# A PSUM bank set aside for the running sum of the convolution taps

## The chip, the core and the metric

The kernel runs on one core of a Trainium2 chip. TensorE (PE) multiplies matrices into PSUM; VectorE (DVE), ScalarE (ACT) and GpSimd (POOL) work on tiles of 128 partitions; SyncE (SP) issues the transfers. Each engine takes its instructions in a fixed order and waits at semaphores for others. The metric is the device time of one execution in microseconds; lower is better.

## What is computed

One layer of a diffusion block over 512 tokens of width 1024, in float32, with 256 context tokens. Cut to what matters here:

```python
def conformer_conv(conv_in, w_dw, b_dw, ln_g, ln_b, w_pw):
    a, g = jnp.split(conv_in, 2, axis=-1)
    u = a * jax.nn.sigmoid(g)
    u = depthwise_conv(u, w_dw, width=31) + b_dw        # 1024 channels, one filter each
    return jax.nn.silu(layer_norm(u, ln_g, ln_b)) @ w_pw

def block(x, ctx, ...):
    hx = modulate(rms_norm(x), ...)                     # adaLN
    conv_x, qa, kva, kr, gates = split(hx @ w_in)
    att = softmax(q @ k.T) @ v                          # 8 heads, low-rank q and kv, rotary part
    x = x + m * ((sig(g1) * conv(conv_x) + sig(g2) * att @ w_o) @ w_out)
    return rms_norm(x + m2 * swiglu(modulate(rms_norm(x))))
```

The 31-tap depthwise convolution of conv_x and the eight heads of attention are independent of each other until the branches are merged.

## The kernel before

Activations lie transposed: 128 channels on the partitions, 512 tokens along the free axis, so 1024 channels are eight tiles. Every product of matrices is made of three matmuls (mm3), since weights and activations are split into a high and a low part; the high part is copied out of PSUM by ACT and the low part is the difference, taken by DVE (split, L103 to L105; split_scaled, L99 to L101, for the queries). Weights are split in the same way: w_hi on ACT (L121), w_lo on DVE (L125).

PSUM has eight banks. ps_s takes two pairs of them for the scores. ps_x takes the other four in rotation, for everything else.

The program opens with a part in an order written out by hand (to about 140 us). Then come the heads (L755 to L773). Head h makes its scores and softmax (scores, p), in between the matmuls of one convolution tile (conv_steps: g and a into two ps_x banks, then u = a*sigmoid(g) on DVE, L333), then prepares the next head (prep: queries into px, split by L100 and L101; keys kx and context keys kc into px, split by L104 and L105; in even heads also the rotary part and the values), then attends (attend): for six blocks of keys four transposes of p into a bank pt (L486), its split into ph and pl, and three matmuls into the bank po.

The taps of convolution tile i (conv_taps) stand in the source with a priority lowered by 3000 (later, L80), so the scheduler places them where an engine would else be free; the order it arrives at is then fixed. Five tiles go over ACT (a scaled copy per tap, L351, three buffers) and POOL (the sum, L352). The tiles 1, 4 and 7 (DVE_TILES) go over DVE alone: L344 begins the sum, 29 instructions of L346 carry it on in a PSUM bank acc, and the last one writes it to the SBUF slot a:

```python
acc = ps_x() if i in DVE_TILES else a
```

That bank comes out of the rotation of ps_x. After the heads come the gates, the normalisation of the convolution, the merging, and the feed-forward part. ap is the pool of SBUF slots for activations; its 60 slots are handed out by slot().

Of the kernel before, what the change touches and what calls it, by code (L numbers as in the profile page):

```python
# [10 lines left out]
F32 = mybir.dt.float32  # L11
# [7 lines left out]
P = 128  # L19
# [27 lines left out]
DVE_TILES = (1, 4, 7)  # L47
# [14 lines left out]
def block_kernel(ctx: ExitStack, tc: tile.TileContext, I, out):  # L62
# [2 lines left out]

    cp = ctx.enter_context(tc.tile_pool(name="cp", bufs=1))
    wp = ctx.enter_context(tc.tile_pool(name="wp", bufs=3))
    ap = ctx.enter_context(tc.tile_pool(name="ap", bufs=60))
    tp = ctx.enter_context(tc.tile_pool(name="tp", bufs=3))
    sm = ctx.enter_context(tc.tile_pool(name="sm", bufs=4))  # L70
    bp = ctx.enter_context(tc.tile_pool(name="bp", bufs=4))
    pp = ctx.enter_context(tc.tile_pool(name="pp", bufs=1, space=PSUM))
# [3 lines left out]
    def nm(s):  # L76
        count[0] += 1
        return f"{s}{count[0]}"
# [7 lines left out]
    def slot(dt=F32, n=512):  # L86
        return ap.tile([P, n], dt, tag="act", name=nm("a"))
# [66 lines left out]
    def v(name, i=None, n=1):  # L154
        a, b = VEC[name]
        return vec[:, a:b] if i is None else vec[:, a + i:a + i + n]
# [21 lines left out]
    def spread(r, nb, psp):  # L178
        dg = temp(nb * P)
        dve.tensor_tensor(  # L180
            out=dg.rearrange("p (b j) -> p b j", b=nb),
            in0=ident.unsqueeze(1).to_broadcast([P, nb, P]),
            in1=r.unsqueeze(2).to_broadcast([P, nb, P]), op=ALU.mult)
        bc = psp(nb * P)
        pe.matmul(bc, lhsT=ones, rhs=dg, start=True, stop=True)
        return bc
# [4 lines left out]
                      start=first and b == 0, stop=last and b == nb - 1)  # L191

    def ps_x(n=512):
        return pp.tile([P, 512], F32, tag="x", name=nm("px"), bufs=4)[:, 0:n]

    def ps_s():
        return pp.tile([P, 1024], F32, tag="s", name=nm("ps"), bufs=2)
# [47 lines left out]


    ab = (ps_s(), ps_s())
    accx = [ab[j // 2][:, (j % 2) * 512:(j % 2) * 512 + 512] for j in range(4)] + [ps_x(), ps_x()]
    tiny = ps_x

    def slab(k, kc):
# [83 lines left out]
    def conv_taps(i, u):  # L335
        a = slot()
        conv[i] = a
        acc = ps_x() if i in DVE_TILES else a
        for j in range(TAPS):
            wcol = wdw[:, i * TAPS + j:i * TAPS + j + 1]  # L340
            src = u[:, j:j + S]
            if i in DVE_TILES:
                if j == 0:
                    dve.tensor_scalar(out=acc, in0=src, scalar1=wcol, scalar2=v("b_dw", i), op0=ALU.mult, op1=ALU.add)  # L344
                else:
                    dve.scalar_tensor_tensor(out=a if j == TAPS - 1 else acc, in0=src, scalar=wcol, in1=acc, op0=ALU.mult, op1=ALU.add)  # L346
            elif j == 0:
                act.activation(a, src, AF.Identity, scale=wcol, bias=v("b_dw", i))
            else:
                t = bp.tile([P, S], F32, tag="tap", name=nm("tap"), bufs=3)  # L350
                act.activation(t, src, AF.Copy, scale=wcol)  # L351
                pool.tensor_tensor(out=a, in0=a, in1=t, op=ALU.add)  # L352
# [164 lines left out]
    with tc.manual_schedule(engines={ET.PE, ET.DVE, ET.Activation, ET.Pool, ET.SP}):  # L517
# [26 lines left out]
        bc = spread(r, 4, tiny)  # L544
# [73 lines left out]
            return dg  # L618

        def bcast(dg, n):  # L620
            bc = tiny(n)
            pe.matmul(bc, lhsT=ones, rhs=dg, start=True, stop=True)
            o = slot(n=n)
            act.copy(o, bc)
            return o
# [125 lines left out]
    with later(TAPS_LATER):  # L751
        conv_taps(0, u0)
        conv_taps(1, u1)
# [24 lines left out]
    if True:  # L778
# [22 lines left out]
        for h in range(H):  # L801
            a, b = slot(F32R), slot(F32R)
            split(o_t[h], a, b)
            oa.append((a, b))
        bc = spread(rstd_cols(st, D, 4), 4, ps_x)
        yc = []
        for i in range(KD):
# [3 lines left out]
            a, b = slot(F32R), slot(F32R)  # L811
# [12 lines left out]
        for i in range(KD):  # L824
# [6 lines left out]
            a, b = slot(F32R), slot(F32R)  # L831
# [197 lines left out]
        i = KD - 1  # L1029
# [139 lines left out]
```

## Time and profile before

| | us |
|---|---|
| median of three runs | 1095.37 (1094.88 to 1096.67) |
| the profiled execution, its time | 1095.09 |
| its span | 1093.3 |
| PE busy | 972.0 |
| DVE busy | 640.0 |
| ACT busy | 525.4 |
| POOL busy | 283.8 |

The span is the time between the first and the last instruction that the profiler recorded; 1.8 us of the execution's time lie outside it. Busy time is the time in which an engine had at least one instruction under way. For matmuls the end is modelled, so the row of PE says where it had nothing at all to do and not how full it was.

### The profile page before, as it was taken

The page shows a single profiled execution, that of the slowest core. Times are in us where ns is not written, and L with a number is a line of the kernel's source. Part 1 is how long each engine was busy: PE and PEld are TensorE (multiplying, and loading weights), DVE is VectorE, ACT ScalarE, POOL GpSimd, SP SyncE. Part 2 cuts the span into 40 slices and gives each one's busy share as a digit, 9 for nine tenths or more (in the row PEclk, how much of TensorE's full clock was granted, in tenths as well). Part 3 has the DMA queues.
Part 4 walks back from the last instruction along what each step waited for, and adds up shares of the span by engine and source line. Part 5 has one row for each costly group of instructions (what it writes and reads, how often), then busy time and mean ns, then how long its engine had stood idle before and what let it go on. Part 6 is the DMA issues. An engine that isn't in the chain of part 4 may idle for free.

```text
span 1093.3 us, 13176 instructions
## 1 busy us (share of the span) xinstructions
PE 972.0 (89%) x4772; PEld 812.0 (74%) x4772; DVE 640.0 (59%) x1052; ACT 525.4 (48%) x963; POOL 283.8 (26%) x237
## 2 busy tenths in 40 slices
PE   8789990988199962999999999999999999999996
PEld 8677880766187752777887888988888888888886
DVE  6997894465846568443589686483653333333333
ACT  4566686888168971554437223353333323332222
POOL 3766168998109991000000000020000000000000
PEclk9889995989599995999999999999999999999998
DMA  9801320011011000123363865133542223333312
GB/s 340 295 20 47 97 74 28 13 58 29 19 32 39 22 20 0 39 95 98 97 211 121 262 205 198 63 99 99 178 133 100 98 86 96 92 95 98 106 54 78
DMA packets 40721, 107.54 MB, mean 98 GB/s; under 512 B 4432, under 2 KB 6736, under 8 KB 40656
## 3 DMA queue, kind: packets, MB, share of 16 engines
q1 hardware_dynamic: 40656, 106.70, 30.3%
q8 instruction: 37, 0.61, 0.2%
q14 instruction: 28, 0.23, 0.1%
HBM read 104.59 MB, written 2.10 MB: 98 GB/s over the span
## 4 chain that ended last, share of the span: by engine, by line
PE 65%; DVE 13%; POOL 8%; ACT 8%; issue 5%; DMA 0%; POOLq 0%; SPq 0%; DVEq 0%; ACTq 0%
PE px L137 12%; PE px L138 11%; PE px L139 11%; POOL a L352 8%; PE ps L138 7%; PE ps L139 7%; PE ps L137 7%; DVE px L346 4%; DVE gm L263 2%; ACT tap L351 2%; PE ps L468 2%; DVE wl L125 2%; ACT p L477 1%; PE px L319 1%; ACT p L474 1%
## 5 line engine op out<-in xcount | busy, mean ns | idle before, releaser
L125 DVE TENSOR_TENSOR wl<-wr,wh 128x512 fp32r<-128x512 f32 (+1 forms) x264 | 197.2, 755 | 238.7 <-ACT wh L121 235.9
L121 ACT CAST wh<-wr 128x512 fp32r<-128x512 f32 (+2 forms) x274 | 164.5, 608 | 295.0 <-PE px L138 141.8
L137 PE MATMUL px<-a,wh 128*128 128x512 f32 (+1 forms) x607 | 224.2, 371 | 1.6 <-DVE t L417 1.0
L352 POOL TENSOR_TENSOR a<-a,tap 128x512 f32<-128x512 f32 x150 | 202.1, 1348 | 86.3 <-ACT tap L351 58.9
L138 PE MATMUL px<-a,wh 128*128 128x512 f32 (+1 forms) x607 | 223.1, 368 | 1.2 <-DVE a L722 1.1
L139 PE MATMUL px<-a,wl 128*128 128x512 f32 (+1 forms) x607 | 222.7, 367 | 0.0
L175 POOL TENSOR_TENSOR s<-s,mhalf 128x2 f32<-128x2 f32 (+1 forms) x10 | 9.3, 932 | 687.5 <-DVE s L173 687.5
L138 PE MATMUL ps<-a,wh 128*128 128x512 f32 (+1 forms) x376 | 141.6, 376 | 0.9 <-DVE a L921 0.8
L137 PE MATMUL ps<-a,wh 128*128 128x512 f32 (+1 forms) x376 | 141.5, 376 | 0.0
L139 PE MATMUL ps<-a,wl 128*128 128x512 f32 (+1 forms) x376 | 141.2, 375 | 0.0
L137 PEld LDWEIGHTS px<-a,wh 128*128 128x128 f32 x607 | 114.3, 188 | 22.1 <-ACT a L104 1.5
L138 PEld LDWEIGHTS px<-a,wh 128*128 128x128 f32 x607 | 114.4, 188 | 21.7 <-DVE a L722 2.0
L139 PEld LDWEIGHTS px<-a,wl 128*128 128x128 f32 x607 | 114.3, 188 | 18.9
L351 ACT ACTIVATE tap<-u,wdw 128x512 f32<-128x512 f32 x150 | 105.1, 722 | 33.8 <-POOL a L352 30.0
L138 PEld LDWEIGHTS ps<-a,wh 128*128 128x128 f32 x376 | 70.7, 188 | 14.3 <-DVE a L921 1.5
L319 PE MATMUL px<-a,wh 128*128 128x512 f32 x256 | 80.7, 393 | 0.0
L139 PEld LDWEIGHTS ps<-a,wl 128*128 128x128 f32 x376 | 70.8, 188 | 12.8
L137 PEld LDWEIGHTS ps<-a,wh 128*128 128x128 f32 x376 | 70.8, 188 | 12.6
L468 PE MATMUL ps<-a,a 128*128 128x512 f32 x160 | 60.1, 411 | 12.8 <-ACT a L104 12.8
L486 PE MATMUL px<-cst,p 128*128 128x128 f32 x192 | 30.7, 288 | 42.6 <-DVE a L346 42.2
L346 DVE SCALAR_TENSOR_TENSOR px<-u,wdw,px 128x512 f32<-128x512 f32 x87 | 65.6, 754 | 2.7
L486 PEld LDWEIGHTS px<-cst,p 128*128 128x128 f32 x192 | 25.2, 150 | 47.6 <-DVE a L346 42.6
(196 smaller groups left out, 1436.2 us busy)
## 6 DMA issues: line engine op xcount, KB each, us to landing
wr<-in_w_dram SPq DMA_DIRECT2D x60, 512.0 KB, 3.5
wr<-in_w_in_dram SPq DMA_DIRECT2D x35, 512.0 KB, 3.6
p<-in_w_mod_dram SPq DMA_DIRECT2D x64, 256.0 KB, 4.1
a<-in_w_mod_dram SPq DMA_DIRECT2D x32, 256.0 KB, 5.7
wr<-in_w_o_dram SPq DMA_DIRECT2D x8, 512.0 KB, 5.2
wr<-in_w_pw_dram SPq DMA_DIRECT2D x8, 512.0 KB, 5.6
wr<-in_w_out_dram SPq DMA_DIRECT2D x8, 512.0 KB, 3.7
a<-in_xT_dram SPq DMA_DIRECT2D x13, 256.0 KB, 5.6
```

Of the source, the lines that this page charges most:

```text
L121: act.copy(h, raw[:, i * WB:i * WB + h.shape[-1]])
L125: (eng or dve).tensor_tensor(out=l, in0=raw[:, i * WB:i * WB + h.shape[-1]], in1=h.bitcast(F32), op=ALU.subtract)
L137: pe.matmul(ps, lhsT=wh, rhs=ah, start=first, stop=False)
L138: pe.matmul(ps, lhsT=wh, rhs=al, start=False, stop=False)
L139: pe.matmul(ps, lhsT=wl, rhs=ah, start=False, stop=last)
L263: dve.scalar_tensor_tensor(out=gm[k], in0=slab(k, kc), scalar=sc[:, kc:kc + 1], in1=gm[k], op0=ALU.mult, op1=ALU.add)
L319: pe.matmul(ps, lhsT=l, rhs=r, start=k == 0 and i == 0, stop=k == n - 1 and i == 2)
L346: dve.scalar_tensor_tensor(out=a if j == TAPS - 1 else acc, in0=src, scalar=wcol, in1=acc, op0=ALU.mult, op1=ALU.add)
L351: act.activation(t, src, AF.Copy, scale=wcol)
L352: pool.tensor_tensor(out=a, in0=a, in1=t, op=ALU.add)
L468: pe.matmul(s[:, 0:512], lhsT=l[:, q0:q0 + P], rhs=rx_, start=i == 0, stop=i == 4)
L486: pe.transpose(pt[:, qb * P:(qb + 1) * P], ps_[qb][:, kb * P:(kb + 1) * P], ident)
```

## The change

A second PSUM tag, c, gets one bank (ps_c), and the tag x of ps_x keeps three instead of four. Three users go to the new bank: the running sum of the taps of the tiles 1, 4 and 7, the last of the six sums of the opening projection (accx[5]), and the four broadcasts in the part written by hand (bcast). The pool of activations has 64 slots instead of 60.

```diff
-    ap = ctx.enter_context(tc.tile_pool(name="ap", bufs=60))
+    ap = ctx.enter_context(tc.tile_pool(name="ap", bufs=64))
...
     def ps_x(n=512):
-        return pp.tile([P, 512], F32, tag="x", name=nm("px"), bufs=4)[:, 0:n]
+        return pp.tile([P, 512], F32, tag="x", name=nm("px"), bufs=3)[:, 0:n]
+
+    def ps_c():
+        return pp.tile([P, 512], F32, tag="c", name=nm("pc"))
...
-    accx = [...] + [ps_x(), ps_x()]
+    accx = [...] + [ps_x(), ps_c()]
...
-        acc = ps_x() if i in DVE_TILES else a
+        acc = ps_c() if i in DVE_TILES else a
...
         def bcast(dg, n):
-            bc = tiny(n)
+            bc = ps_c()[:, 0:n]
```

No instruction is added or removed. The scheduler orders the heads anew, and the lines behind L194 move down by three (L346 becomes L349, L486 becomes L489).

DVE at tile 4, in head 2. u_2388 is the tile's input, px_2503 (then pc_2503) its running sum, wl the low parts of weights, px_2545, px_2559 and px_2570 the query, key and context key of head 3. Before:

```order
L333 SCALAR_TENSOR_TENSOR u_2388<-t_2462,px_2464 128x512
L125 TENSOR_TENSOR wl_2775<-wr_2770,wh_2773 128x512
L344 TENSOR_SCALAR px_2503<-u_2388,wdw,vec 128x512
L346 SCALAR_TENSOR_TENSOR px_2503<-u_2388,wdw,px_2503 128x512 x5
L125 TENSOR_TENSOR wl_2903<-wr_2899,wh_2901 128x512
L125 TENSOR_TENSOR wl_2904<-wr_2899,wh_2902 128x512
L346 SCALAR_TENSOR_TENSOR px_2503<-u_2388,wdw,px_2503 128x512 x24
L346 SCALAR_TENSOR_TENSOR a_2502<-u_2388,wdw,px_2503 128x512
L101 SCALAR_TENSOR_TENSOR a_2556<-px_2545,a_2555 128x512
L105 TENSOR_TENSOR a_2567<-px_2559,a_2566 128x512
```

And now:

```order
L336 SCALAR_TENSOR_TENSOR u_2388<-t_2462,px_2464 128x512
L347 TENSOR_SCALAR pc_2503<-u_2388,wdw,vec 128x512
L125 TENSOR_TENSOR wl_2775<-wr_2770,wh_2773 128x512
L349 SCALAR_TENSOR_TENSOR pc_2503<-u_2388,wdw,pc_2503 128x512 x3
L125 TENSOR_TENSOR wl_2903<-wr_2899,wh_2901 128x512
L125 TENSOR_TENSOR wl_2904<-wr_2899,wh_2902 128x512
L349 SCALAR_TENSOR_TENSOR pc_2503<-u_2388,wdw,pc_2503 128x512 x26
L349 SCALAR_TENSOR_TENSOR a_2502<-u_2388,wdw,pc_2503 128x512
L101 SCALAR_TENSOR_TENSOR a_2556<-px_2545,a_2555 128x512
L105 TENSOR_TENSOR a_2567<-px_2559,a_2566 128x512
```

Two of the taps moved from ahead of the second and third weight split to behind them; the splits of query and key stand behind the last tap in both.

ACT at tile 1, in head 0. tap are the scaled copies that POOL sums, a_1679 begins the sum of tile 2, a_1791 is the high part of the next query, a_1802 and a_1813 those of the keys, ph_1822 that of the first transposed block. Before:

```order
L351 ACTIVATE tap_1684<-u_1565,wdw 128x512
L351 ACTIVATE tap_1687<-u_1565,wdw 128x512
L348 ACTIVATE a_1679<-u_1565,vec,wdw 128x512
L100 ACTIVATE a_1791<-px_1781 128x512
L104 CAST a_1802<-px_1795 128x512
L104 CAST ph_1822<-px_1817 128x512
L104 CAST a_1813<-px_1806 128x256
L351 ACTIVATE tap_1690<-u_1565,wdw 128x512
```

And now:

```order
L354 ACTIVATE tap_1684<-u_1565,wdw 128x512
L351 ACTIVATE a_1679<-u_1565,vec,wdw 128x512
L100 ACTIVATE a_1791<-px_1781 128x512
L354 ACTIVATE tap_1687<-u_1565,wdw 128x512
L104 CAST a_1802<-px_1795 128x512
L354 ACTIVATE tap_1690<-u_1565,wdw 128x512
L104 CAST a_1813<-px_1806 128x256
L354 ACTIVATE tap_1693<-u_1565,wdw 128x512
L104 CAST ph_1822<-px_1817 128x512
```

One tap moved from ahead of a_1679 and of the query's copy to behind them, and taps now stand between the copies that follow.

DVE at tile 7, in head 5. t_3683 and t_3685 are the rotary products of head 6's query (px_3673), pl their low parts. Before:

```order
L344 TENSOR_SCALAR px_3631<-u_3516,wdw,vec 128x512
L125 TENSOR_TENSOR wl_4004<-wr_3999,wh_4002 128x512
L346 SCALAR_TENSOR_TENSOR px_3631<-u_3516,wdw,px_3631 128x512
L417 TENSOR_TENSOR t_3683<-px_3673,cst 128x512
L417 TENSOR_TENSOR t_3685<-px_3673,cst 128x512
L346 SCALAR_TENSOR_TENSOR px_3631<-u_3516,wdw,px_3631 128x512
L105 TENSOR_TENSOR pl_3688<-t_3683,ph_3687 128x512
L105 TENSOR_TENSOR pl_3692<-t_3685,ph_3691 128x512
L125 TENSOR_TENSOR wl_4005<-wr_3999,wh_4003 128x512
L346 SCALAR_TENSOR_TENSOR px_3631<-u_3516,wdw,px_3631 128x512 x27
L346 SCALAR_TENSOR_TENSOR a_3630<-u_3516,wdw,px_3631 128x512
L101 SCALAR_TENSOR_TENSOR a_3706<-px_3695,a_3705 128x512
```

And now:

```order
L125 TENSOR_TENSOR wl_4004<-wr_3999,wh_4002 128x512
L347 TENSOR_SCALAR pc_3631<-u_3516,wdw,vec 128x512
L420 TENSOR_TENSOR t_3683<-px_3673,cst 128x512
L420 TENSOR_TENSOR t_3685<-px_3673,cst 128x512
L349 SCALAR_TENSOR_TENSOR pc_3631<-u_3516,wdw,pc_3631 128x512
L105 TENSOR_TENSOR pl_3688<-t_3683,ph_3687 128x512
L105 TENSOR_TENSOR pl_3692<-t_3685,ph_3691 128x512
L125 TENSOR_TENSOR wl_4005<-wr_3999,wh_4003 128x512
L349 SCALAR_TENSOR_TENSOR pc_3631<-u_3516,wdw,pc_3631 128x512 x28
L349 SCALAR_TENSOR_TENSOR a_3630<-u_3516,wdw,pc_3631 128x512
L101 SCALAR_TENSOR_TENSOR a_3706<-px_3695,a_3705 128x512
```

One tap moved from ahead of the rotary low parts to behind them.

## Rows read from the trace of the kernel before

**Rows 1.** Page, busy us, share of the span, instructions of each engine

```profile
PE 972.0 (89%) x4772; PEld 812.0 (74%) x4772; DVE 640.0 (59%) x1052; ACT 525.4 (48%) x963; POOL 283.8 (26%) x237
```

**Rows 2.** Waits: who waited for whom; us in total, times, longest

```profile
PE px L486 <- DVE a L346: 42.2, 2, 27.4
PE px L432 <- DVE a L346: 28.5, 1, 28.5
...
PE ps L468 <- ACT a L104: 12.8, 2, 11.3
```

**Rows 3.** Windows: length, busy PE, PEld, DVE, ACT, POOL, granted clock, DMA share, GB/s

```profile
163.00:178.00 15.00, 0.24 (x2) 0.13 (x2) 12.30 (x16) 8.80 (x13) 14.21 (x11) 0.64 0.20 66
...
268.60:296.30 27.70, 0.32 (x3) 0.11 (x1) 24.84 (x33) 5.16 (x9) 8.70 (x9) 0.58 0.13 38
402.50:431.00 28.50, 0.07 (x1) 0.00 (x0) 25.14 (x32) 7.46 (x13) 12.24 (x9) 0.57 0.00 0
```

**Rows 4.** Page, groups of instructions: busy us, mean ns, idle before, releaser

```profile
L352 POOL TENSOR_TENSOR a<-a,tap 128x512 f32<-128x512 f32 x150 | 202.1, 1348 | 86.3 <-ACT tap L351 58.9
...
L346 DVE SCALAR_TENSOR_TENSOR px<-u,wdw,px 128x512 f32<-128x512 f32 x87 | 65.6, 754 | 2.7
```

**Rows 5.** Timeline of ACT at tile 1: start, length, instruction, idle before

```profile
186.53 0.72 ACT L351 ACTIVATE tap<-u,wdw 128x512 f32<-128x512 f32 x1 [0.62 <-POOL u L331]
187.87 0.72 ACT L351 ACTIVATE tap<-u,wdw 128x512 f32<-128x512 f32 x1 [0.62 <-POOL a L352]
188.50 0.80 ACT L348 ACTIVATE a<-u,vec,wdw 128x512 f32<-128x512 f32 x1
189.20 0.57 ACT L100 ACTIVATE a<-px 128x512 fp32r<-128x512 f32 x1
```

**Rows 6.** Timeline of POOL behind tile 1

```profile
189.37 21.73 POOL L352 TENSOR_TENSOR a<-a,tap 128x512 f32<-128x512 f32 x16 [1.45 <-ACT a L348]
211.55 8.50 POOL L352 TENSOR_TENSOR a<-a,tap 128x512 f32<-128x512 f32 x6 [0.45 <-ACT tap L351]
221.10 10.85 POOL L352 TENSOR_TENSOR a<-a,tap 128x512 f32<-128x512 f32 x7 [1.04 <-ACT tap L351]
```

**Rows 7.** Timeline of ACT at the end of head 0

```profile
207.65 0.92 ACT L477 ACTIVATE p<-p,s 128x768 f32<-128x768 f32 x1
...
210.70 1.32 ACT L351 ACTIVATE tap<-u,wdw 128x512 f32<-128x512 f32 x2
```

**Rows 8.** Timeline of DVE at tile 4

```profile
268.50 3.92 DVE L346 SCALAR_TENSOR_TENSOR px<-u,wdw,px 128x512 f32<-128x512 f32 x5
274.21 2.36 DVE L125 TENSOR_TENSOR wl<-wr,wh 128x512 fp32r<-128x512 f32 x2 [1.79 <-ACT wh L121]
276.50 19.02 DVE L346 SCALAR_TENSOR_TENSOR px<-u,wdw,px 128x512 f32<-128x512 f32 x24
...
296.22 0.69 DVE L101 SCALAR_TENSOR_TENSOR a<-px,a 128x512 fp32r<-128x512 f32 x1
296.82 1.01 DVE L105 TENSOR_TENSOR a<-px,a 128x512 fp32r<-128x512 f32 x2
```

**Rows 9.** Timeline of DVE at tile 7

```profile
404.83 2.36 DVE L105 TENSOR_TENSOR pl<-t,ph 128x512 fp32r<-128x512 f32 x2 [2.62 <-ACT ph L104]
...
408.79 21.39 DVE L346 SCALAR_TENSOR_TENSOR px<-u,wdw,px 128x512 f32<-128x512 f32 x27
...
430.88 0.68 DVE L101 SCALAR_TENSOR_TENSOR a<-px,a 128x512 fp32r<-128x512 f32 x1
...
441.20 0.69 DVE L105 TENSOR_TENSOR pl<-px,ph 128x512 fp32r<-128x512 f32 x1 [2.11 <-ACT ph L104]
```

**Rows 10.** Windows between and behind the stalls, columns as in Rows 3

```profile
297.00:402.00 105.00, 101.52 (x511) 83.07 (x510) 59.13 (x84) 84.03 (x146) 68.71 (x51) 0.98 0.10 30
...
431.00:500.00 69.00, 66.46 (x339) 53.79 (x340) 32.99 (x54) 37.23 (x73) 0.00 (x0) 0.96 0.18 61
...
540.00:700.00 160.00, 159.37 (x745) 132.41 (x744) 122.08 (x246) 64.92 (x122) 1.02 (x1) 1.00 0.56 184
```

More of the change, by code (lines that the diff above doesn't have):

```diff
@@ L247, in block_kernel @@
     ab = (ps_s(), ps_s())
-    accx = [ab[j // 2][:, (j % 2) * 512:(j % 2) * 512 + 512] for j in range(4)] + [ps_x(), ps_x()]
+    accx = [ab[j // 2][:, (j % 2) * 512:(j % 2) * 512 + 512] for j in range(4)] + [ps_x(), ps_c()]
     tiny = ps_x
```

## The prediction

> **What bounds the kernel now.** I began with the busy times of the page: PE 89% of the span [rows 1], so the question is where PE has nothing to do. The table of waits answers it in three rows [rows 2]: PE waited 42.2 us at the transposes of attend (L486, twice, the longest 27.4, so the other 14.8) and 28.5 us at the rotary sum (L432, once), and in all three cases the releaser is the last tap of a DVE tile (L346). That is 14.8 + 27.4 + 28.5 = 70.7 us. A fourth row, 11.3 us at the scores for a copy on ACT, follows directly on the first of them. The windows [rows 3] show the three stretches, at tile 1 (163 to 178 us), tile 4 (268.6 to 296.3) and tile 7 (402.5 to 431): PE does next to nothing, DVE is busy nearly throughout (24.84 of 27.7 us in the second), and the granted clock is 0.57 to 0.64 of full, near the lower of its two levels (1.2 of 2.4 GHz). The reader is to see two things there. Before, the taps hold one of four rotating banks; the queries, keys and context keys of the next head hold the other three; the next transpose needs a fifth. And DVE is not waiting for anybody: it is working off 24 to 27 taps in a row.
>
> The third view is the order of the instructions, shown with the change. It decides the case: the bank is not all that PE lacks. The query's low part (L101) and the keys' low parts (L105), which free the other three banks, stand on DVE behind the last tap, before and now. Whatever bank the taps use, no bank of the rotation comes free until DVE is through with them.
>
> Between the stalls POOL sets the pace: a tap costs it 1348 ns [rows 4], ACT has only three tap buffers and so runs in step with it (two taps on ACT start 187.87 - 186.53 = 1.34 us apart, each after a wait for POOL) [rows 5], and ACT's other work, which PE needs, stands among the taps.
>
> **The change part by part.** No instruction is added or removed, so everything is order and waiting.
>
> *The three stalls stay.* PE's first step behind the taps now needs the bank of the query px_2545 (at tile 4), which is free after L101, one instruction behind the last tap. From the start of L101 to the start of the next instruction on DVE is 296.82 - 296.22 = 0.60 us [rows 8]. So the wait for L346 becomes one for L101, 0.6 us longer, at tiles 4 and 7. It costs nothing less, for DVE has the same taps to do; what would shorten it is only taps that DVE does sooner.
>
> *Tile 4: taps done later.* Two taps that stood ahead of two weight splits now stand behind them. Those splits wait for ACT (1.79 us idle before 274.21) [rows 8], so the taps ahead were free, and behind they are not: 2 x 19.02/24 = 1.6 us. With L101: +2.2 us. The bounds: +0.6, if the splits come as much earlier as the taps are fewer, and +2.2 plus 1.8 if ACT's copies come later by another such wait.
>
> *Tile 7.* One tap moved behind the two rotary low parts, before which DVE waited 2.62 us for ACT [rows 9]; so it leaves a free place for a paid one: 21.39/27 = 0.8 us. With L101: +1.4 us (bounds +0.6 and +2.2).
>
> *Tile 1.* Here ACT, not DVE, is last: the query's copy L100 stands behind the taps and the beginning of tile 2's sum (L348) and runs at 189.20 [rows 5]; it is what the 11.3 us at the scores [rows 2] end with. POOL meanwhile waits 1.45 us for L348 [rows 6]. Now one tap fewer stands ahead of both, one step of POOL: L348 at 188.50 - 1.34 = 187.16. That takes 1.3 us out of POOL's chain, which leads to the splits before tile 4's taps; the copies behind L100 now have taps between them, so PE gains nothing of its own. -1.3 us (bounds -1.45 and 0).
>
> *The ends of heads 0, 3 and 4.* The copies of the last transposed blocks now stand behind three to seven more taps, and then ACT has its softmax work in one bunch instead of parted by taps. The longest run without a tap was 210.70 - 207.65 = 3.05 us at the end of head 0 [rows 7]; now the last copy, two exponentials, the copy of the result, two scalings and a weight copy stand together, which by the lengths seen there is about 5.2 us, longer than three buffered taps last POOL (3 x 1.35 = 4.05). Before, POOL's gaps there were 0.45 and 1.04 us [rows 6]. I estimate gaps larger by 5.2 - 4.05 = 1.2 us, of which the taps that now come sooner give back some two thirds: +0.45 us each, 3 x 0.45 = +1.35 us (bounds -1 and +4).
>
> *Two banks for the transposes instead of three* in the heads without a tap sum (with one, it was two already, since the taps held the other). A block's bank is free after its low part on DVE, 0.69 us [rows 9]. All of it exposed in the 42 blocks of heads 1 to 7 would be 29 us; none of it, 0. The new order puts scores and convolution matmuls between the blocks, which hide it; only the last heads have none left. I take the near end, 0.1 us in each of seven blocks: +0.7 us.
>
> The Trainium skill speaks against this part: Perfetto Trace Analysis, section Matmul Optimizations, wants all eight PSUM banks leveraged, and the new bank lies idle outside the taps and the four broadcasts. By that rule the part would cost something in every stage that rotates banks, not 0.7 us; by the row of 540 to 700 us [rows 10] PE is busy 159.37 of 160 us with groups of 24 matmuls per bank, so three banks leave the evacuation far more room than it needs there.
>
> *No cost:* the opening part written by hand has the same order but for two taps that now precede the last key splits, and before, DVE made them up in free places; accx[5] and the broadcasts share one bank in turns where they took turns in the rotation. Its cover is the matmuls of the values; without it, two taps, 2 x 0.754 = 1.5 us [rows 4]. The four extra slots and six moved rows on SP lie in stages in which PE is full [rows 10].
>
> The sum: 2.2 + 1.4 - 1.3 + 1.35 + 0.7 = +4.35 us. The profiled execution took 1095.09 us (span 1093.3 and 1.8 around it), 0.3 below the median of 1095.37. 1095.1 + 4.4 = 1099.5 us.
>
> **The rivals.**
>
> *The stalls go, as the bank suggests.* PE would do the transposes while DVE does the taps. All of the 70.7 us [rows 2] would make 1024 us; half, 1060. For it: the releaser named is L346. Against it: L101 behind the last tap in the order, at all three tiles. It would need a bank that frees without DVE. The Trainium skill has a rule for this side: Perfetto Trace Analysis, section Optimization Strategy, says that consistent bubbles can mean that there isn't enough PSUM to allocate the next tile. By it the bubbles should shrink when the taps' bank leaves the rotation; but the rotation shrinks by the same bank, and the rows name an engine that was at work. Chance 4%.
>
> *Not slower: matmuls fill the waits.* The new order on PE puts scores and convolution matmuls between transposes and products. PE's idle time that this can fill is 105 - 101.52 = 3.5 us in 297 to 402 and 69 - 66.46 = 2.5 us in 431 to 500 [rows 10], 6.0 in all. If it fills more than 4.35 us of it, the change is not slower; all of it gives 1099.5 - 6.0 = 1093.5 us. Against it: in the first stretch POOL's chain (POOL busy 68.71 of 105) paces ACT, and PE's idle time only moves. Chance 26% that it ends within 0.2%, 9% that it ends faster.
>
> *Two banks are too few.* If a quarter of the 29 us is exposed, +7 us: 1106.5; all of it, 1128. For it: ACT's copies now stand behind more taps, so a block's bank is held longer. Against: PE has other work ordered in between. Chance 9% for above 1105.5.
>
> **How the numbers follow.** A measurement of this kernel can tell about 0.2%, 2.2 us. The forecast, slower by 2.2 to 10 us, has 52%; with the third rival 61% for slower. Within 0.2%: 26%. Faster: 9 + 4 = 13%. The range leaves 9% above and about 10% below: 1094.0 to 1105.5. Its ends come from the bounds: the two fills short of complete below, and the upper bounds of tile 4 (+1.8), tile 7 (+0.8) and the heads' ends (+2.7) above, 1099.5 + 5.3 = 1104.8, rounded up.
>
> **What would show it.** Right: waits of PE for DVE L101 of about 28 us twice, at the transposes and the rotary sum, and none for L349; DVE busy with 26 and 28 taps ahead of each; POOL's wait for the beginning of tile 2's sum gone; a larger gap of POOL at the ends of heads 0, 3 and 4. Wrong: PE busy during the taps of tile 4 or 7; PE's waits at transposes for the previous block's low part adding to more than 5 us; the span of 500 us on changed by more than 1 us; or tile 4's splits coming at another time than 273 to 275 us.

## The result, and the profile after

The changed kernel took 1114.09 us (median of 4 runs, 1111.0 to 1117.17) against 1096.02 for the kernel before: 1.0166 times as long, 95% interval 1.0133 to 1.0198. That is +18 us where +4.4 was forecast, and outside the range of 1094.0 to 1105.5. The profiled execution is the shortest of the four, 1111.0 us, with a span of 1109.2 us: 15.9 more than before. Lines 195 and up of the old numbering are three higher now: the taps are L349, POOL's additions L355, the transposes L489, the rotary sum L435.

Of the page, the busy times, and of the groups the products whose idle time grew most and the transposes (busy us, mean ns, idle before, releaser):

```profile
PE 973.2 (88%) x4772; PEld 810.4 (73%) x4772; DVE 637.0 (57%) x1052; ACT 525.7 (47%) x963; POOL 283.5 (26%) x237
...
L137 PE MATMUL px<-a,wh 128*128 128x512 f32 (+1 forms) x607 | 225.9, 373 | 5.9 <-ACT t L331 4.5
...
L489 PE MATMUL px<-cst,p 128*128 128x128 f32 x192 | 32.7, 287 | 50.2 <-DVE a L101 49.5
```

No engine has noticeably more work than in [rows 1] (PE 1.2 us and ACT 0.3 more, DVE 3.0 and POOL 0.3 less), so nearly all of the difference is waiting. PE's waits (us in total, times, longest):

```profile
PE px L489 <- DVE a L101: 49.5, 3, 26.4
PE px L435 <- DVE a L101: 24.7, 3, 18.5
PE px L137 <- ACT ph L104: 15.1, 11, 2.7
PE ps L471 <- ACT a L104: 11.3, 2, 7.3
...
PE px L137 <- ACT t L331: 4.5, 1, 4.5
```

Read against [rows 2]: the waits for the last tap are gone by name and are there by size. Before, 42.2 + 28.5 = 70.7 us were waited for L346; now 49.5 + 24.7 = 74.2 us for L101, the instruction behind the last tap. These two sums are not quite the same waits: 7.0 of the 74.2 us (4.5, 1.7 and 0.8) lie in other places, and the wait at the scores for ACT, 11.3 us at tile 1 before [rows 2], now stands ahead of the waits at tiles 4 and 7. These are PE's rows there:

```profile
281.79 0.50 PE L471 MATMUL ps<-a,a 128*128 128x512 f32 x1 [4.03 <-ACT a L104]
304.62 1.11 PE L489 MATMUL px<-cst,p 128*128 128x128 f32 x4 [22.32 <-DVE a L101]
...
425.08 0.80 PE L471 MATMUL ps<-a,a 128*128 128x512 f32 x1 [7.31 <-ACT a L104]
444.40 0.80 PE L435 MATMUL px<-ph,stackr 128*128 128x512 f32 x1 [18.52 <-DVE a L101]
```

Counted by stall, with the scores, tile 1 has 26.4 us (before 14.8 + 11.3 = 26.1), tile 4 has 4.0 + 22.3 = 26.3 (27.4) and tile 7 has 7.3 + 18.5 = 25.8 (28.5). In PE's table one row has grown, that for the copies of the transposed blocks (ph) in the heads, to 15.1 us, and one is new, 4.5 us, once, for an activation of the opening. Of ph the table of the kernel before has:

```profile
PE px L137 <- ACT ph L104: 4.1, 6, 1.4
```

The windows of the three stalls (length, busy PE, PEld, DVE, ACT, POOL, granted clock, DMA share, GB/s) answer to [rows 3]:

```profile
163.00:194.00 31.00, 4.64 (x24) 3.81 (x23) 17.49 (x22) 19.56 (x31) 29.33 (x27) 0.62 0.12 34
276.00:304.00 28.00, 2.26 (x12) 1.58 (x10) 25.39 (x34) 4.35 (x9) 7.54 (x7) 0.63 0.12 37
414.00:444.00 30.00, 4.57 (x21) 3.35 (x19) 28.28 (x38) 7.71 (x13) 12.72 (x9) 0.65 0.00 0
```

Nearly the same picture: PE does little and the clock is 0.62 to 0.65. At tiles 4 and 7 DVE is at its taps. At tile 1 it is through with them at 181.6 us and waits, like PE, for the query's copy on ACT (L100):

```profile
193.03 0.69 DVE L101 SCALAR_TENSOR_TENSOR a<-px,a 128x512 fp32r<-128x512 f32 x1 [11.44 <-ACT a L100]
```

At tile 4 the timeline of DVE answers to [rows 8], 7.7 us later at L101 and 6.1 later where the weight splits end and the long row of taps begins:

```profile
276.41 2.33 DVE L349 SCALAR_TENSOR_TENSOR pc<-u,wdw,pc 128x512 f32<-128x512 f32 x3
282.57 20.60 DVE L349 SCALAR_TENSOR_TENSOR pc<-u,wdw,pc 128x512 f32<-128x512 f32 x26
...
303.88 0.68 DVE L101 SCALAR_TENSOR_TENSOR a<-px,a 128x512 fp32r<-128x512 f32 x1
```

**Where the 15.9 us come from.** The eight executions of L101, one for each head, are good milestones: their starts are read from the timelines of DVE in both traces, and behind the heads the first product of the channel sums (L786, now L789) and the first gated product of the last part (L871, now L874).

| milestone | before | after | later by | added in this step |
|---|---|---|---|---|
| L101 of head 0 (end of the opening) | 130.1 | 134.3 | 4.2 | 4.2 |
| L101 of head 1 (tile 1) | 189.8 | 193.0 | 3.2 | -1.0 |
| L101 of head 2 (end of head 0) | 230.7 | 237.2 | 6.5 | 3.3 |
| L101 of head 3 (tile 4) | 296.2 | 303.9 | 7.7 | 1.2 |
| L101 of head 4 (end of head 2) | 331.0 | 339.6 | 8.6 | 0.9 |
| L101 of head 5 (end of head 3) | 368.6 | 381.0 | 12.4 | 3.8 |
| L101 of head 6 (tile 7) | 430.9 | 443.7 | 12.8 | 0.4 |
| L101 of head 7 | 461.6 | 471.4 | 9.8 | -3.0 |
| first product of the channel sums | 539.1 | 551.5 | 12.4 | 2.6 |
| first gated product | 733.3 | 749.5 | 16.2 | 3.8 |
| end | 1093.3 | 1109.2 | 15.9 | -0.3 |

The steps with the stalls add 1.2 + 0.4 and give back 1.0; that of tile 4 also holds the end of head 1, that of tile 7 the end of head 4. Most of what is won up to head 7 is given back in the next step. What costs is the opening, the heads between the stalls, and a stretch behind the heads in which PE was full and nothing was to change.

**The opening.** PE's order is the same there, and yet it waits 4.53 us for the activation of L331. This is PE's row, then ACT's, of the changed kernel:

```profile
119.69 0.58 PE L137 MATMUL px<-a,wh 128*128 128x256 f32 x1 [4.53 <-ACT t L331]
```

```profile
118.64 0.51 ACT L722 ACTIVATE a<-t,s 128x256 fp32r<-128x256 f32 x1 [0.28 <-DVE t L719]
119.06 0.58 ACT L331 ACTIVATE t<-px 128x512 f32<-128x512 f32 x1
```

The product (line 730, the context's keys and values) needs a bank. Before, a fourth one was free. Now the three of the rotation are taken, and the first to come free is read by an activation that stands on ACT behind those of the context (L722). The separate bank lies idle.

**The end of head 0.** PE, in the changed kernel, waits at the products with ph:

```profile
200.56 0.50 PE L137 MATMUL px<-ph,a 128*128 128x512 f32 x1 [1.28 <-ACT ph L104]
...
206.00 0.50 PE L137 MATMUL px<-ph,a 128*128 128x512 f32 x1 [1.85 <-ACT ph L104]
...
212.81 0.50 PE L137 MATMUL px<-ph,a 128*128 128x512 f32 x1 [2.40 <-ACT ph L104]
```

ACT at the same time (three rows of one period):

```profile
199.31 0.72 ACT L354 ACTIVATE tap<-u,wdw 128x512 f32<-128x512 f32 x1 [0.64 <-POOL a L355]
199.94 1.05 ACT L104 CAST ph<-px 128x512 fp32r<-128x512 f32 x2
200.88 0.73 ACT L354 ACTIVATE tap<-u,wdw 128x512 f32<-128x512 f32 x1
```

Two copies come together, then four or five taps, each in step with POOL, then the next copies: two blocks are as many as two banks hold.

### The profile page after: what moved, and what is told of

Its sections match the earlier page's. It is cut to its first block, busy times and chain, and to the rows that moved or that the text cites. A ratio compares the mean times of both kernels' runs of the same rounds, so it can differ in the third digit from the quotient of the medians.

```text
span 1109.2 us, 13168 instructions
## 1 busy us (share of the span) xinstructions
PE 973.2 (88%) x4772; PEld 810.4 (73%) x4772; DVE 637.0 (57%) x1052; ACT 525.7 (47%) x963; POOL 283.5 (26%) x237
## 4 chain that ended last, share of the span: by engine, by line
PE 56%; DVE 15%; POOL 10%; ACT 7%; issue 7%; DMA 4%; POOLq 0%; DVEq 0%; SPq 0%; ACTq 0%
POOL a L355 9%; PE px L137 9%; PE px L138 9%; PE px L139 9%; PE ps L138 7%; PE ps L137 7%; PE ps L139 7%; DMA p<-in_w_mod_dram 4%; DVE pc L349 4%; DVE gm L266 2%; PE px L322 2%; DVE wl L125 2%; PE ps L471 2%; ACT tap L354 1%; DVE a L216 1%
## 5 line engine op out<-in xcount | busy, mean ns | idle before, releaser
L125 DVE TENSOR_TENSOR wl<-wr,wh 128x512 fp32r<-128x512 f32 (+1 forms) x264 | 193.3, 740 | 244.0 <-ACT wh L121 240.9
L355 POOL TENSOR_TENSOR a<-a,tap 128x512 f32<-128x512 f32 x150 | 201.8, 1346 | 94.8 <-ACT tap L354 67.7
L137 PEld LDWEIGHTS ps<-a,wh 128*128 128x128 f32 x376 | 70.8, 188 | 12.8
L489 PE MATMUL px<-cst,p 128*128 128x128 f32 x192 | 32.7, 287 | 50.2 <-DVE a L101 49.5
L471 PE MATMUL ps<-a,a 128*128 128x512 f32 x160 | 62.0, 418 | 11.3 <-ACT a L104 11.3
L349 DVE SCALAR_TENSOR_TENSOR pc<-u,wdw,pc 128x512 f32<-128x512 f32 x87 | 65.6, 754 | 2.7
L489 PEld LDWEIGHTS px<-cst,p 128*128 128x128 f32 x192 | 25.0, 147 | 57.0 <-DVE a L101 50.2
```

The lines of the kernel that those rows point to most:

```text
L125: (eng or dve).tensor_tensor(out=l, in0=raw[:, i * WB:i * WB + h.shape[-1]], in1=h.bitcast(F32), op=ALU.subtract)
L137: pe.matmul(ps, lhsT=wh, rhs=ah, start=first, stop=False)
L471: pe.matmul(s[:, 0:512], lhsT=l[:, q0:q0 + P], rhs=rx_, start=i == 0, stop=i == 4)
L489: pe.transpose(pt[:, qb * P:(qb + 1) * P], ps_[qb][:, kb * P:(kb + 1) * P], ident)
```

## The experiments

**Theory A**: the price is the fourth bank that the rotation lost, wherever it was used. **Theory B**: the planner's other order of copies and taps on ACT is the price, whatever the banks. **Theory C**: the 64 slots. Beside these stood a question of its own: whether the stalls of 70.7 us need a bank at all, or another place for L101.

**64 slots alone**

```diff
-    ap = ctx.enter_context(tc.tile_pool(name="ap", bufs=60))
+    ap = ctx.enter_context(tc.tile_pool(name="ap", bufs=64))
```

> The kernel before with 64 activation slots in place of 60 and nothing else; four banks stay in rotation and the sum stays in one of them. Theory A (the missing fourth bank costs the time): within 2 us of the kernel before, about 1094 to 1098. Theory B (the planner's new order of the copies and taps on ACT costs it, whatever the banks): also near the kernel before, since the order hardly moves here. Theory C (more slots let loads and splits run earlier and collide): +10 to +18 us, since nothing else of the change is left.

1093.52 us, ratio 0.9967 (0.9956 to 0.9979): a small gain that none of the theories had. The milestones up to tile 7 lie within 0.3 us of before; L101 of head 7 comes at 459.8 in place of 461.6 us. C falls.

**The opening repaired**, on the changed kernel

```diff
-        pkv = ps_x()
+        pkv = ps_c()
...
-        bc_c = bcast(dg_c, C)
+        bc_c = bcast(dg_c, C, ps_x)
```

> The changed kernel with one product of the opening (the context's keys and values, line 730) put into the separate bank, which lies idle then, and its one broadcast that would collide put into the rotation. The PE wait of 4.5 us for the ACT copy of L331 at 119 us should go. Theory A: 4.0 to 5.0 us less than the changed kernel, about 1109.5, because PE has no other gap there and the POOL chain of the taps, which starts 4.6 us late, starts on time. Theory B: the opening doesn't matter, PE catches up later: within 1 us of the changed kernel, about 1114.

1109.63 us, 4.5 less. The product finds its bank; PE's longest wait there, now for its data, is about that of the kernel before (0.72):

```profile
117.91 0.39 PE L138 MATMUL pc<-a,wh 128*128 128x256 f32 x1 [0.78 <-DVE a L725]
```

In the profiled executions less is left of it: L101 of head 0 comes 2.3 us earlier (132.0), that of head 1 1.7, and at tile 4 nothing (304.2); from 118 to 126 us both had a granted clock of 0.79 (the kernel before 1.00), and from 195 to 240 us this execution had 0.88 where the other had 0.96. The medians speak for A; how much of the 4.5 us is the wait and how much the clock of those runs, they don't separate.

**The sum in SBUF, four banks** (on the kernel before) **and three** (on the changed kernel)

```diff
-        acc = ps_x() if i in DVE_TILES else a
+        acc = a
```

> The kernel before, but the running sum of the three tiles stands in the SBUF slot that receives the result anyway; four banks are all in rotation and none is held for a sum. Theory A: no price for a missing bank, and the three long waits of PE stay, now for L101 behind the taps on DVE: 1090 to 1098, near the kernel before. Theory B (a planner's order with the sums out of the rotation is itself worse): +8 to +14 us, about 1104 to 1110. A third reading, that the waits of 70.7 us go once no bank is tied up: 1024 to 1060. If a tap with its sum in SBUF is slower or faster than 756 ns, 87 of them move the stalls by that.

> The changed kernel, but the running sums stand in the SBUF slot as in the run before this one; the separate bank serves only the opening, so the heads have three banks and the eighth lies idle. Theory A: as the changed kernel, 1111 to 1118, since the count in rotation is the same; the difference to the run with four banks is the price of the fourth bank, +14 to +20 us. Theory B: what the run with four banks gives, since the sums are out of the rotation in both, plus the 4.5 us of the opening at most.

1066.95 and 1080.98 us. Both are faster than the kernel before (0.9728, 0.9712 to 0.9744; 0.9866, 0.9843 to 0.9888), which no theory had said; only the difference came out, 14.0 us for the fourth bank. The timeline of DVE at tile 4, with four banks, shows what changed there:

```profile
281.33 3.31 DVE L346 SCALAR_TENSOR_TENSOR a<-u,wdw,a 128x512 f32<-128x512 f32 x2
284.57 0.68 DVE L101 SCALAR_TENSOR_TENSOR a<-px,a 128x512 fp32r<-128x512 f32 x1
285.17 1.15 DVE L346 SCALAR_TENSOR_TENSOR a<-u,wdw,a 128x512 f32<-128x512 f32 x1
```

L101 stands behind three taps in place of all 31, and the rest fill DVE's gaps over the next 58 us. The planner ordered it so once the sum was in SBUF; the source does not ask for it. PE's waits for L101 or the last tap, 70.7 us before, are 18.4 us at tile 1 and 3.5 elsewhere. That made a theory of the open question: the stalls come from the place of L101, and a kernel that puts it ahead of the taps should win without any of this.

**The same with 64 slots**, four banks

> The sums in the SBUF slot and four banks in rotation, with 64 slots in place of 60. The 64 slots alone gave 3.3 us. Theory A (slots act by themselves): 1062 to 1066. Rival: what they gave belongs to one place that the other order of the taps has removed: 1066 to 1068.

1065.80 us against 1066.95: no difference that these runs can tell, and on the border of the two ranges. Whether what the slots gave belongs to the old order stays open.

**The taps held back behind L101**, on the changed kernel. The taps of tiles 1, 4 and 7 are cut in two; the second part's first weight is made from the query's low part (times zero, plus the weight, so that its value stays and it only has to wait):

```diff
+    accs, CUT = {}, {1: 18, 4: 3, 7: 3}
...
+            if part == 1 and j == CUT[i]:
+                z = small(1, "gate")
+                dve.tensor_scalar(out=z, in0=ev[:, 0:1].bitcast(F32), scalar1=0.0, scalar2=wcol, op0=ALU.mult, op1=ALU.add)
+                wcol = z
...
+            with later(TAPS_LATER):
+                conv_taps(i, u1 if h == 0 else u, 1, qn[h + 1][1])
```

> The changed kernel, banks and slots as in it, but the taps of tiles 1, 4 and 7 are cut in two and the second part (from tap 18, 3 and 3) reads its first weight from a small DVE operation that needs the low part of the next head's query (L101), so that L101 can't stand behind those taps. Theory A (two separate things: the waits of 70 us come from L101's place behind the taps in DVE's row, and the missing fourth bank costs its 18 us beside that): the waits for L101 of 26.4 and 18.5 us go nearly whole and that of tile 1 in part, the taps fill DVE's gaps, ACT's waits for ph stay near 15 us: 1060 to 1085. Theory B (the taps have no room beside the heads: whatever stands behind them waits as long): 1105 to 1116, with the waits now for L105.

1079.52 us, 35 less than the changed kernel, with the bank and the slots as they were. The wait at tile 4 is gone (0.9 us left) and that at tile 7 is 9.2 us, while two waits for L101 at rotary sums grew to 6.0 and 6.3 us (4.5 and 1.7); at these tiles the bank was not what PE lacked. The 26.4 us that A let go nearly whole stand at tile 1, and 23.7 of them stay: L101 there waits 16.5 us for L100 on ACT, which this cut does not touch. The waits for ph stay (11.9 us), as A has it.

**The heads' output sum in the idle bank**, on the sum in SBUF with three banks

```diff
-        po = ps_x()
+        po = ps_c()
```

> The sums in the SBUF slot and three banks in rotation (1081 us), but each head's output sum po (line 485) stands in the separate bank that lies idle there, so that the transposes of the head rotate over three banks in place of two. Theory A (two banks for the transposes make PE wait for ph in the heads): the 13.4 us of waits for ph fall below 7 and the time by 6 to 10 us, 1071 to 1075; the 4.5 us of the opening stay. Theory B (only the planner's order counts): 1078 to 1083.

1072.29 us, 8.7 less than 1080.98: the transposes have three banks instead of two, and PE's waits for ph fall from 13.4 to 2.0 us. A.

**The same in the changed kernel**, in the six heads in which no tap needs the bank

```diff
-        po = ps_x()
+        po = ps_c() if h in (0, 1, 3, 4, 6, 7) else ps_x()
```

It ran beside the changed kernel itself and the next repair.

> The changed kernel itself once more, so that the two runs beside it are compared with it on one chip: 1111 to 1116 by the four times that it gave (1111.0 to 1117.2). If its larger spread comes from TensorE's granted clock after the stalls, the times follow the mean clock of each run.

> The changed kernel, but the output sum po of heads 0, 1, 3, 4, 6 and 7 stands in the separate bank, which no tap sum needs in those heads; the transposes there have three banks in place of two, and the taps keep their place. Theory A (two banks for the transposes cost the heads what is left of the difference): waits of PE for ph from 15 to below 8 us and 5 to 9 us less than the changed kernel, 1105 to 1109. Theory B (the price in the heads comes from ACT's order, copies behind more taps, which stays nearly as it is): within 2 us of the changed kernel.

1114.45 and 1101.25 us: 13.2 less, more than expected (10.1 in the two profiled spans, 1110.3 and 1100.2). Of the changed kernel's eight times the shortest (1111.0) has the highest mean clock, 0.949, and the longest (1117.2) 0.941, so its spread goes with the clock, as far as eight runs show. PE's waits with the repair, first those for L101, hardly changed, then the scores, then ph:

```profile
PE px L489 <- DVE a L101: 50.1, 3, 26.4
PE px L435 <- DVE a L101: 25.1, 3, 17.2
PE ps L471 <- ACT a L104: 16.0, 2, 11.1
...
PE pc L137 <- ACT ph L104: 1.1, 2, 0.8
```

The waits for ph fell by 13.9 us (15.0 before the repair), but 4.7 of these came back at the scores, which had 11.3. POOL's gap at the end of head 0 fell, too. First the changed kernel, then the repaired one; before it was 0.45 us [rows 6]:

```profile
218.02 8.49 POOL L355 TENSOR_TENSOR a<-a,tap 128x512 f32<-128x512 f32 x6 [2.40 <-ACT tap L354]
```

```profile
218.21 8.49 POOL L355 TENSOR_TENSOR a<-a,tap 128x512 f32<-128x512 f32 x6 [0.57 <-ACT tap L354]
```

This run does not refute B's mechanism: with a third bank the planner also set ACT's copies ahead of more taps, one or two at a time, where the changed kernel has two, two and one, behind three to five taps each. ACT in head 0 of the repaired kernel:

```profile
197.83 0.56 ACT L104 CAST ph<-px 128x512 fp32r<-128x512 f32 x1
198.54 0.72 ACT L354 ACTIVATE tap<-u,wdw 128x512 f32<-128x512 f32 x1 [0.15 <-POOL a L355]
199.17 0.57 ACT L104 CAST ph<-px 128x512 fp32r<-128x512 f32 x1
```

So the bank and the order changed together. That the bank decides the order, and the order on ACT is how its price is paid, is a reading of the rows and not shown by itself. What a copy that stands early would give with two banks was not tried.

**Four banks again behind the heads**

```diff
+            if turn[0] % 4 == 0:
+                return ps_c()[:, 0:n]
...
+    turn.append(0)
     for i in range(3, KD):
         gate_mla(i, o_t[6])
```

> The changed kernel; behind the heads (from 500 us on) every fourth tile of PSUM takes the separate bank, so that four banks rotate there again. From 540 to 735 us (first product of the channel sums, L786, to the first gated product, L871) the kernels with four banks took 194 to 195 us and those with three 197 to 198. Theory A (the bank is missed there too): 2.5 to 4 us less than the changed kernel, with 194 to 195 us in that stretch. Rival (a clock that varies by chance): within 1 us of it.

1109.56 us, 4.9 less. From the first product of the channel sums to the first gated product this execution needs 750.25 - 556.12 = 194.1 us, like the kernel before (194.2), and the changed kernel beside it 196.7. So 2.6 us are this stretch's; the rest of the 4.9 is not shown to be the bank's, and the two profiled spans differ by 0.6 us only (1109.7 and 1110.3), since this execution was 1.7 us later at L101 of head 0, where the kernels are the same. All profiles agree on the stretch: the seven of kernels with three banks there need 195.9 to 198.0 us, the nine with four 194.1 to 195.0. The bank's price there is 1.7 to 3.8 us over 194.2. The two rows, of PE and of DVE (this kernel's lines are seven higher still):

```profile
556.12 1.02 PE L796 MATMUL pc<-a,ones 128*128 128x512 f32 x2
```

```profile
750.25 0.68 DVE L881 TENSOR_TENSOR t<-ps,t 128x512 f32<-128x512 f32 x1
```

**All three repairs**

> The changed kernel with the three repairs at once: the opening's product and the heads' output sums in the separate bank where it is idle, and four banks in rotation behind the heads; the taps keep the bank while they run, and their order stays. Alone the three gave 4.5, 13.2 and 4.9 us of the changed kernel's 1114.3. Theory A (the missing bank is the whole price and the three places add up): 1091 to 1095, the time of the kernel before with 64 slots (1093.5). Rival (the repairs overlap, since a late opening is caught up in the stall of tile 1): 1096 to 1101, and some of the price is then not the bank's.

1097.59 us, 16.9 less than the changed kernel; against the kernel before 1.0008 (0.9997 to 1.0019). With the bank at work where it was idle, the time is back at that of the kernel before. It lies in the rival's range, though: the three don't add up (4.5 + 13.2 + 4.9 = 22.6), and against the kernel with the same 64 slots (1093.5) 4 us are left. The rival's reason is in the rows, but small: from L101 of head 0 to that of head 1 the kernels with the opening repaired take 59.3 and 59.4 us, the others with three banks and the taps in their old order 58.7, so the stall of tile 1 takes back 0.6 us.

From L101 of head 0 to the channel sums this execution runs nearly like that with the slots alone (408.9 and 407.3 us); it is late by 3.3 us before. At 74 us the two are level (the weight split L125 starts at 74.05 and 74.04). 1.9 us are lost between 72 and 90 us and 1.5 between 118 and 126, and there the granted clock differs. Windows of 72 to 90 us, the slots alone and then the repaired kernel:

```profile
72.00:90.00 18.00, 14.98 (x76) 12.01 (x77) 14.43 (x21) 14.00 (x32) 12.60 (x10) 1.00 0.20 60
```

```profile
72.00:90.00 18.00, 16.75 (x67) 13.54 (x67) 10.18 (x18) 13.45 (x30) 11.22 (x10) 0.81 0.17 60
```

PE is busy for longer and does fewer matmuls, at a clock between its two levels in place of the upper one. From 118 to 126 us the clocks are 1.00 and 0.79; three kernels with four banks (sums in SBUF and 64 slots, with and without cut taps) have 0.79 there, too, so this second dip is not the missing bank's. The first one stands in six of the nine profiles of kernels whose rotation has three banks there (0.72 to 0.88, the changed kernel in one of its two) and in none of the seven with four (0.91 to 1.00). That makes it likelier that the three banks bring it about, but no run shows how. The twelve times of the repaired kernel fall into 1095.5 to 1096.2 and 1097.3 to 1100.0.

**The order alone**, on the kernel before: four banks, the sum in one of them, 64 slots, and only the cut taps of above

> The kernel before with its four banks in rotation and the sums in one of them, with 64 slots, and only the taps of tiles 1, 4 and 7 cut and held back behind L101. Theory A (the stalls of 70.7 us come from the order on DVE, not from the bank that the sum holds): the waits at tiles 4 and 7 go without any bank of their own for the sum, 1062 to 1078. Rival (the bank matters more than the order: a sum that is held through the heads leaves them three banks): the heads pay the 13 us that the changed kernel paid, 1078 to 1092.

1069.46 us, 0.9748 (0.9731 to 0.9765): the stalls of tiles 4 and 7 shrink without a bank for the sum, and it is 10 us faster than the same order with a bank of its own (1079.5). Of 27.4 and 28.5 us, waits of 5.2 and 5.9 us are left about tile 4, and 5.3 and 7.8 about tile 7. In each pair the second is for the last tap itself (L353), so the bank that the sum holds is still felt, by 13.7 us. The stall of tile 1 stays, as it did with the cut taps above:

```profile
PE px L493 <- DVE a L101: 28.6, 2, 23.4
...
PE px L137 <- DVE a L353: 7.8, 1, 7.8
```

**A faster kernel.** The cut taps with the sum in SBUF, four banks and 64 slots:

> The sums in the SBUF slot, four banks in rotation, 64 slots, and the taps of the three tiles cut and held back behind L101 as in the first run of this set. Theory A: the wait of 18.4 us for L101 at tile 1, the one that is left with the sums in SBUF, goes in good part: 1048 to 1060. Rival: the last taps of tile 1 run beside POOL's, where a tap in SBUF takes 1.68 us in place of 0.75, and the heads wait behind them in other places: 1062 to 1068, as without the cut.

1063.46 us, 0.97 (0.9673 to 0.9728), so the time is the rival's, but not its reason. L101 of head 1 was no longer behind taps on DVE; it waited for its first half on ACT:

```profile
194.62 0.69 DVE L101 SCALAR_TENSOR_TENSOR a<-px,a 128x512 fp32r<-128x512 f32 x1 [15.95 <-ACT a L100]
```

L100 stands on ACT behind tile 0's taps. The last run cuts those as well:

```diff
+                if i in DVE_TILES:
+                    dve.tensor_scalar(out=z, in0=ev[:, 0:1].bitcast(F32), scalar1=0.0, scalar2=wcol, op0=ALU.mult, op1=ALU.add)
+                else:
+                    act.activation(z, ev[:, 0:1].bitcast(F32), AF.Identity, scale=0.0, bias=wcol)
...
+                if h == 0:
+                    conv_taps(0, u0, 1, qn[1][0])
```

> The run with the sums in SBUF, four banks, 64 slots and the cut taps (1063.5 us), in which PE still waits 15.0 us at tile 1 for L101, and that for the ACT copy of L100 in a row behind some 20 products of tile 0's taps, each paced by a POOL addition of 1.35 us. Here tile 0's taps are cut at tap 10 and the rest is held behind that copy. Theory A (an in-order row with taps ahead of a copy that PE needs is what stalls, on ACT as on DVE): the wait falls below 4 us and the time to 1048 to 1056. Rival: POOL's chain of additions, 20 of them later by some 15 us, becomes the end of the taps and moves the wait to the sum of the channels behind the heads: 1060 to 1066.

1056.79 us, 0.9646 (0.9627 to 0.9665), the fastest of all; 0.8 above the expected range. The wait of 15.0 us at tile 1 is gone; one for the next head's L101 (L381) rose from 4.7 to 8.5 us:

```profile
PE px L381 <- DVE a L101: 8.5, 1, 8.5
PE ps L597 <- ACT a L581: 6.9, 6, 2.1
PE px L138 <- DVE pl L105: 5.6, 6, 2.0
```

## Why the prediction was right in sign and wrong in size

- *The three stalls stay*: right. With the waits at the scores they were 82.0 us and are 78.5, and the releaser is L101, as the order said. The cut taps, with and without the bank, show that L101's place behind DVE's taps was the cause at tiles 4 and 7. At tile 1 it was L100's place behind the taps on ACT, as the prediction's part on tile 1 had it: that stall went only when ACT's taps were cut, too.
- *Tile 4 (+2.2), tile 7 (+1.4), tile 1 (-1.3)*: measured +1.2, +0.4 and -1.0 by the milestones, which are the starts of L101 and so leave out the 0.6 us that L101 itself adds at tiles 4 and 7. PE goes on 8.3 us later than before at tile 4 (304.62 against 296.36) and 13.3 later at tile 7 (444.40 against 431.11), so that as PE sees them the steps are 0.6 and 0.5 larger: +1.8 and +0.9, within their bounds. The signs are right and the sizes somewhat too large. At tile 4 the mechanism can be read off: from the two weight splits to L101 DVE took 23.6 us in place of 22.0, the 1.6 us of two taps. The single longest waits were not 28 us twice, as announced, but 22.3 and 18.5 at tiles 4 and 7, since PE now stops at the scores first and does a few matmuls in between.
- *Ends of heads 0, 3 and 4 (+1.35) and two banks for the transposes (+0.7)*: these two terms failed. Together they were 2.05 us; the milestones of the heads show 3.3 + 0.9 + 3.8 = 8.0 us, and the repair in the changed kernel gave 10.1 in the spans. I had priced them apart: the banks by the 0.69 us that a block's bank is held at its end, with other matmuls to hide it, and the bunches on ACT by what POOL's buffers cover. The rows point to one mechanism. With two banks the copies go two at a time; between them ACT is in step with POOL, so a copy that misses its place waits for several taps of 1.35 us, and PE behind it, in order, can't do the matmuls that were to hide it. What the bunches cost was mis-sized, too: POOL's gaps at the ends of heads 0, 3 and 4 are 2.40, 2.46 and 2.41 us in place of 0.45, 0.45 and 0.67, so 1.7 to 2.0 more each, where the forecast had 1.2 and, after what was given back, 0.45. The bunch had its forecast length (212.19 to 217.16 is 4.97 us, for 5.2). Its cover was taken too long: POOL had work for 3.4 us from the start of the bunch, not for three taps (4.05), and could go on only 0.9 us after the first new tap had started on ACT. ACT, then POOL, in the changed kernel:

```profile
212.19 0.56 ACT L104 CAST ph<-px 128x512 fp32r<-128x512 f32 x1
...
217.16 1.33 ACT L354 ACTIVATE tap<-u,wdw 128x512 f32<-128x512 f32 x2
```

```profile
192.59 23.02 POOL L355 TENSOR_TENSOR a<-a,tap 128x512 f32<-128x512 f32 x17
```

The rows of the kernel before could have told it: a run of 3.05 us without a tap [rows 7] already left a gap of 0.45 us [rows 6], so 5.2 us had to leave some 2.6. How much of the 8.0 us came through PE's waits for ph and how much through POOL's later chain, no run separates. The upper bound of 29 us did hold the price.

- *No cost in the opening*: failed, 4.2 us, of which the repair gave back 2.3 in the profiles; the rest stands where the clock was lower. I took an order that hardly changed for a cost that hardly changed, and counted the users of the separate bank, not those of the three that were left.
- *No cost from 500 us on*: failed, 3.8 us in the profiled execution, 2.6 by the repair, 1.7 to 3.8 in all profiles with three banks there. The row that I rested on [rows 10] says that PE was busy 159.37 of 160 us with four banks; it doesn't say what three would do. The Trainium skill's rule that I had set against it (Perfetto Trace Analysis, section Matmul Optimizations: all eight PSUM banks are to be leveraged) came out right in each of the three places where the bank lay idle: using it there gave 4.5, 13.2 and 4.9 us.
- *The rivals*: "two banks are too few" was the one that happened, with a chance of 9%, and it named one place of three. "Matmuls fill the waits" was seen behind tile 7: 3.0 us were won in that step, of which 2.6 were given back in the next; with the slots alone 1.8 were won and kept. "The stalls go" did not happen with the bank; with another order those of tiles 4 and 7 went or shrank to waits of 5 to 9 us.
- *What would show it wrong*: the line on 500 us on named the failure before it happened, and the one on waits at the transposes asked for the wrong releaser (the low part on DVE; it was the copy on ACT). Tile 4's splits came at 280.29 us, outside the 273 to 275 announced, since all ahead of them was late; from L101 of head 2 they are 0.4 us nearer than before. Of the signs of being right, POOL's wait for the beginning of tile 2's sum is gone and its gaps at the ends of heads 0, 3 and 4 are larger.

The sum by its terms: opening 4.2 for 0; stalls 0.6 for 2.3; heads 8.0 for 2.05; from head 7 on 3.1 (3.8 behind the channel sums, less 0.7 in the other steps) for 0. In all 15.9 for 4.35.

## What to carry to other kernels

When the profile names a buffer's writer as the releaser, look at what stands behind that writer on its engine before you buy another buffer: here another order of the taps, with the 64 slots, was worth 27 us (the slots alone 3), and the bank bought nothing. A buffer taken out of a rotation costs at every place that rotates, also where the order stays and where the engine looks full; go through those places one by one, and let the new buffer serve where it is idle. Work that is to fill gaps, paced by a slower engine, must not stand ahead of a copy that the critical engine needs, on any in-order engine.

## What the runs showed of the hardware

A tap with its sum in SBUF is as quick as with its sum in PSUM when POOL rests, and more than twice as slow beside POOL's additions; POOL is slower then too. With the sum in SBUF, DVE (18.47/11 = 1.68 us each beside POOL; 0.74 alone), then POOL (31.49/19 = 1.66 us each):

```profile
181.09 18.47 DVE L346 SCALAR_TENSOR_TENSOR a<-u,wdw,a 128x512 f32<-128x512 f32 x11
...
428.71 0.74 DVE L346 SCALAR_TENSOR_TENSOR a<-u,wdw,a 128x512 f32<-128x512 f32 x1
```

```profile
167.52 31.49 POOL L352 TENSOR_TENSOR a<-a,tap 128x512 f32<-128x512 f32 x19 [3.13 <-ACT tap L351]
```

With the sum in PSUM, DVE's taps take 0.754 us and POOL's additions 1.348 in the mean of the whole kernel [rows 4], POOL running or not: ten taps at tile 1, where POOL is busy 14.21 of 15 us [rows 3], take 7.87 us, 0.79 each, like the 27 at tile 7 (21.39 us [rows 9]), most of which run while POOL rests.

```profile
169.17 7.87 DVE L346 SCALAR_TENSOR_TENSOR px<-u,wdw,px 128x512 f32<-128x512 f32 x10
```

The Trainium skill states this contention (SBUF — State Buffer, section Who interferes with whom: a DVE instruction with two SBUF inputs contends with a GpSimd instruction that reads SBUF), and the trace agrees, 1.68 against 0.75 us. The sum in SBUF was still the faster kernel, with the cut taps too (1063.5 against 1069.5 us). That the taps hold no bank there, and that many of them run while POOL rests (27 us at tile 4), fits this; the two were not tried apart.
